# Layer 0's four product groups for the scans by quarters of the contraction beside the modulation, the gate product later, the modulation spread anew

## The chip, the core and the metric

The kernel runs on one core of a Trainium2 chip. The metric is the device time of one execution in microseconds (us), the median over a few executions. A difference of 0.3% (8.7 us) is about what a measurement of this kernel can tell from none.

## The reference, cut to what matters

Two layers run over two groups of 128 tokens each (context and latent) with shared weights; D_MODEL is 2048. The code is cut to the parts that the change touches.

```python
def _modulation(cond, ada_w, ada_b):
    m = jax.nn.silu(cond) @ ada_w + ada_b
    m = m.reshape(cond.shape[0], 1, N_MOD, D_MODEL)
    return [m[:, :, i] for i in range(N_MOD)]
...
def _mixer(h, p, ctx):
    u = h @ p['w_in']
    q, k, v, u_hy, u_rkv, w_dn, a_dn, g_dn = jnp.split(u, IN_SPLITS, axis=-1)
    ...
    hy = _hyena(u_hy, p)
    rw, S_fin = _rwkv(u_rkv, w_dn, a_dn, g_dn, p, S0)
    o = jnp.concatenate([att, hy, rw], axis=-1) @ p['w_out']
...
def _layer(x, cond, p, ctx):
    sh1, sc1, g1, sh2, sc2, g2 = _modulation(cond, p['ada_w'], p['ada_b'])
    nw = p['norm_w']
    h = _rmsnorm(x, nw[0]) * (1.0 + sc1) + sh1
    o, st = _mixer(h, p, ctx)
    x = x + g1 * _rmsnorm(o, nw[1])
    h = _rmsnorm(x, nw[2]) * (1.0 + sc2) + sh2
    f = jnp.square(jax.nn.relu(h @ p['mlp_w1'])) @ p['mlp_w2']
    x = x + g2 * _rmsnorm(f, nw[3])
```

The six modulation vectors of a layer (numbers 0 to 5: sh1, sc1, g1, sh2, sc2, g2) need one 2048 x 12288 weight matrix per layer, 16.8 MB a vector. The scans (`_rwkv`) need r, k, v and the two low-rank inputs of decay and rate (`w_dn`, `a_dn`); the gate input `g_dn` is used only at their end.

## The kernel before, in words

**Products.** A weight is loaded in float32 by SyncE's DMA queue, split by ScalarE (L244) and VectorE (L245) into two halves, and every product is three matmuls: high x high (seen as L165), high x low and low x high (L523 and L524 in `ws`, L542 and L543 in `as_`). `ws` holds the weight still and moves 256 tokens; `as_` holds the tokens still and moves up to 512 weight columns. One load covers two or four of the sixteen 128-row steps of the contraction. `self.run` drives such a group; each of its steps reports its columns, and 6144 columns are one **unit** (24 matmuls of 256 columns).

**Modulation.** `ada_vector` loads one vector as 32 tiles of 512 KB (L394) and multiplies each (L399). One tile with its matmuls is a **step**; a vector has 33 or 34. `ada_push` queues vectors, `run` issues so many steps per unit as `ada_mix` (in the mixer) or `ada_mlp` (in the MLP) says, `drain` issues one whenever the side work has to wait, `ada_until` issues what is left up to a vector, and `ada_step(fill)` issues `fill` more before the residual and norm that follow the mixer of each layer and the MLP of layer 0. Layer 0's vectors 1 and 0 are needed first. `ada_group` computes them in four column groups of 512, and `ada_boot` takes turns between two; the products of one vector's column group are eight tiles of 512 KB (L354, L360).

**Start.** In `build`, each column group of the two vectors releases a quarter of the norm (`norm`, one chunk of `act` per call) and, some steps later (`b1`, `b2`), four contraction steps of the two groups of `mixer_first`: "wa" (four blocks of 96 columns, the low-rank inputs) and "k" of the first half of the heads. These two groups hold the two PSUM buffers of the tag `mm` until the fourth quarter.

**Mixer.** `mixer` then runs, in this order: `rwkv_lora` and the short convolution of k (`conv`, L551 to L553), the gate group (C_G, 256 columns), r and v of the first half, then q, k, v of the attention, r, k, v of the second half, three Hyena groups and the output projection in three phases (attention with heads 0 and 1, Hyena, the rest). The scans are side work: `side.add(rwkv_batch ...)` stands after v; a batch of three pairs of heads goes through `rwkv_kk`, `rwkv_stage1`, `rwkv_invert` (a chain of VectorE steps with two round trips through DRAM), `rwkv_stage2` and `rwkv_out`, and the second batch follows the first. `Side.step` issues pieces of it as units go by. Before each phase of the output projection `drain` issues what the phase still needs. `Beside.queue` pins each side matmul behind the last product matmul issued, so that the planner cannot move it ahead; apart from that the planner orders each engine's queue by program order and by its own estimate of when operands are ready.

**Residual and norm.** After the output projection and after each MLP, `residual` (L1248, L478) and `norm` (L473, L487, L497 to L502) form a chain over VectorE, ScalarE and transposes (L179) before the next product can start.

**Buffers.** Raw weight tiles: four of the tag `wr` (products, and half of the first modulation tiles) and six of `wa` (modulation). Three high and three low halves. `sm` has three PSUM buffers, `mm` two.

Of the kernel before, what the change touches and what calls it, by code (L numbers as in the profile page):

```python
# [33 lines left out]
def _shape_constants():  # L34
# [56 lines left out]
    for k, v in c.items():  # L91
# [16 lines left out]
OPTS = dict(mm_bufs=2, sm_bufs=3, raw=4, araw=6, hi=3, lo=3, t0=16, t1=8, k1=25, k2=15, k4=18, ada_mix=1.0,  # L108
            ada_mlp=0.75, sr=3.5, sq=3, sh=4, so=7, ra=0.3, wa1=1.5, wa2=0.5, w0=1, w1=3, wi=0.5,
            ni=3, w2=0.5, w3=3, w4=2, w5=0.4, fill=8, b1=2, b2=5)  # L110
# [47 lines left out]
class Beside:  # L158


    def __init__(self, tc):
        self.tc, self.last = tc, None

    def main(self, *a, **k):
        i = self.tc.nc.tensor.matmul(*a, **k)  # L165
        self.last = i.ins.name
        return i

    def queue(self, i):
        if self.last is not None:  # L170
            self.tc.add_manual_dep(i.ins, self.last, mybir.DependencyInfo(mybir.DependencyClass.NoSync, mybir.DependencyReason.DATA),
                                   reason="beside")
        return i

    def matmul(self, *a, **k):
        return self.queue(self.tc.nc.tensor.matmul(*a, **k))  # L176

    def transpose(self, *a, **k):
        return self.queue(self.tc.nc.tensor.transpose(*a, **k))  # L179


class Kern:
    def __init__(self, tc, es, A, O, opts=None):
# [7 lines left out]
        self.te = Beside(tc)  # L191
# [8 lines left out]
    def late(self, ins, back=8):  # L200

        if len(self.anchors) > back:
            self.tc.add_manual_dep(ins.ins, self.anchors[-1 - back],
                                   mybir.DependencyInfo(mybir.DependencyClass.Sync, mybir.DependencyReason.DATA), reason="late")
        return ins

# [42 lines left out]
    def setup(self):  # L249
# [17 lines left out]
        self.te.transpose(ps[:, 0:32], th[:], self.ident[0:32, 0:32])  # L267
# [21 lines left out]
    def params(self, l):  # L289
# [34 lines left out]
        for i, gr in enumerate(groups):  # L324
# [3 lines left out]
            self.te.transpose(ps[:, 0:n], rows[:], self.ident[0:n, 0:n])  # L328
# [151 lines left out]
    def norm(self, P, parts, isc, ish, act):  # L480
# [3 lines left out]
        for c in range(4):  # L484
            for g in range(2):
# [4 lines left out]
                for j in range(4):  # L490
                    self.te.transpose(pv[:, j, :], xn[:, j * 128:(j + 1) * 128], self.ident)
# [14 lines left out]
    def ws(self, act, w, widths, ps):  # L506
# [4 lines left out]
        for kq in range(KT // nk):  # L511
            hi, lo = self.wload(w[kq * nk * 128:(kq + 1) * nk * 128, :], nk, ncol)
            for kk in range(nk):
                k = kq * nk + kk
                hh, hl = act[k // 4][0][:, k % 4, :], act[k // 4][1][:, k % 4, :]
                c0 = 0
                for b, wd in enumerate(widths):
                    o = ps[0:wd, b * 256:(b + 1) * 256]
                    h, lw = hi[:, kk, c0:c0 + wd], lo[:, kk, c0:c0 + wd]
                    m = self.te.main(o, lhsT=h, rhs=hh, start=(k == 0 and b % 2 == 0), stop=False, skip_group_check=True)  # L520
# [878 lines left out]
```

## Time and profile before

| | |
|---|---|
| median of three executions | 2912.18 us (2906.03 to 2915.72) |
| the profiled execution | 2905.54 us |
| its span, first to last instruction | 2903.8 us |
| TensorE (matmul) busy | 2798.7 us, 96% |
| VectorE, ScalarE busy | 57%, 42% |
| HBM read | 632.21 MB |

The profile is of one execution. In the view of windows a row gives the length of a stretch, then for each engine its busy time and instruction count, then TensorE's mean granted clock (1.00 is 2.4 GHz, 0.50 is 1.2 GHz), the mean busy share of the DMA engines and what they moved. In the timeline a row gives start, duration, engine, line, operation, output and inputs, shapes and count; the bracket is the time that the engine sat idle before it and what ended that. Each matmul of the modulation is float32 and shows as two instructions, so that one step shows as x4.

### The profile page before, as it was taken

How to read it: one execution, taken by the hardware profiler on the slowest of the kernel's cores; microseconds unless marked ns; L12 is line 12 of the kernel's file. 1: busy time of each engine (PE TensorE's matmuls, PEld its weight loads, DVE VectorE, ACT ScalarE, POOL GpSimd, SP SyncE). 2: the span in 40 equal slices, each digit the busy share in tenths (PEclk: the TensorE clock that was granted, in tenths of full speed). 3: DMA queues.
4: the chain of work that ended last, by engine and by line, in shares of the span. 5: the costliest groups of instructions: out<-in, count | busy, mean ns of one | idle time of the engine just before them, and what ended most of it. 6: DMA issues, size and time to landing. Idle time of an engine off the chain costs nothing. (4 is left out here: it accounts for less than half of the span.)

```text
span 2903.8 us, 47850 instructions
## 1 busy us (share of the span) xinstructions
PE 2798.7 (96%) x19163; PEld 2308.9 (80%) x19163; DVE 1646.6 (57%) x2627; ACT 1232.8 (42%) x1870; POOL 179.1 (6%) x368
## 2 busy tenths in 40 slices
PE   6899999999999999999999999999879999999998
PEld 3586888766897797897876979887669989899896
DVE  1356766776644344444445577677775545555555
ACT  2354445433533343333345454453354444444343
POOL 0011101201000000000000111021000000000000
PEclk8999999999999999999999999998989999999999
DMA  9985764578888888888898745433456666666674
GB/s 334 335 302 192 236 225 153 188 240 289 294 282 288 278 285 277 294 280 282 284 337 286 225 138 143 137 90 111 146 176 184 185 191 184 188 188 187 190 241 150
DMA packets 326057, 654.56 MB, mean 225 GB/s; under 512 B 48581, under 2 KB 86030, under 8 KB 325707
## 3 DMA queue, kind: packets, MB, share of 16 engines
q1 hardware_dynamic: 311328, 610.88, 65.0%
q0 software_dynamic: 12928, 36.98, 3.8%
q8 instruction: 150, 2.46, 0.3%
q10 hardware_dynamic: 1579, 3.64, 0.3%
q14 instruction: 72, 0.59, 0.1%
HBM read 632.21 MB, written 19.20 MB: 224 GB/s over the span
## 5 line engine op out<-in xcount | busy, mean ns | idle before, releaser
L245 DVE TENSOR_TENSOR wl<-wr,wh 128x1024 fp32r<-128x1024 f32 (+1 forms) x784 | 929.1, 1186 | 926.6 <-ACT wh L244 903.2
L244 ACT CAST wh<-wr 128x1024 fp32r<-128x1024 f32 (+1 forms) x784 | 798.6, 1019 | 1188.3 <-PE mm L523 532.9
L165 PE MATMUL mm<-acth,wh 128*128 128x256 f32 (+1 forms) x3200 | 922.0, 288 | 11.8 <-ACT acth L501 8.5
L523 PE MATMUL mm<-actl,wh 128*128 128x256 f32 (+1 forms) x3200 | 906.5, 283 | 0.0
L524 PE MATMUL mm<-acth,wl 128*128 128x256 f32 (+1 forms) x3200 | 904.5, 283 | 1.9 <-DVE wl L245 1.9
L165 PEld LDWEIGHTS mm<-acth,wh 128*128 128x128 f32 (+1 forms) x3200 | 603.6, 189 | 61.0 <-issue 25.2
L524 PEld LDWEIGHTS mm<-acth,wl 128*128 128x128 f32 (+1 forms) x3200 | 604.7, 189 | 7.2 <-DVE wl L245 3.5
L523 PEld LDWEIGHTS mm<-actl,wh 128*128 128x128 f32 (+1 forms) x3200 | 602.4, 188 | 4.1 <-issue 2.7
L165 PE MATMUL mm<-wh,fh 128*128 128x512 f32 x1024 | 405.8, 396 | 0.0
L542 PE MATMUL mm<-wl,fh 128*128 128x512 f32 x1024 | 403.0, 394 | 0.0
L543 PE MATMUL mm<-wh,fl 128*128 128x512 f32 x1024 | 401.6, 392 | 0.0
L165 PEld LDWEIGHTS mm<-wh,fh 128*128 128x128 f32 x1024 | 192.2, 188 | 63.0 <-ACT wh L244 9.2
L543 PEld LDWEIGHTS mm<-wh,fl 128*128 128x128 f32 x1024 | 192.0, 187 | 45.4
L542 PEld LDWEIGHTS mm<-wl,fh 128*128 128x128 f32 x1024 | 192.2, 188 | 42.5 <-DVE wl L245 0.4
L399 PE MATMUL ada<-wa,cs 128*32 128x512 f32 x1280 | 180.0, 607 | 6.7 <-DMA wa<-in_ada_w_dram 6.5
L165 PE MATMUL mm<-wh,osh 128*128 128x512 f32 x256 | 106.4, 416 | 4.9 <-ACT osh L1200 3.4
L542 PE MATMUL mm<-wl,osh 128*128 128x512 f32 x256 | 101.9, 398 | 0.3 <-DVE wl L245 0.3
L399 PEld LDWEIGHTS ada<-wa,cs 128*32 128x32 f32 x1280 | 35.5, 109 | 83.5 <-issue 55.4
L543 PE MATMUL mm<-wh,osl 128*128 128x512 f32 x256 | 101.3, 396 | 0.0
L176 PE MATMUL sm<-rZR,rKB 64*128 64x256 f32 x384 | 76.4, 419 | 1.4 <-DVE rLA L933 1.4
L165 PE MATMUL mm<-wh,acth 128*128 128x512 f32 (+1 forms) x192 | 74.4, 387 | 0.0
L542 PE MATMUL mm<-wl,acth 128*128 128x512 f32 (+1 forms) x192 | 68.8, 358 | 0.0
(319 smaller groups left out, 2566.5 us busy)
## 6 DMA issues: line engine op xcount, KB each, us to landing
wr<-in_mlp_w_dram SPq DMA_DIRECT2D x512, 512.0 KB
wa<-in_ada_w_dram SPq DMA_DIRECT2D x352, 512.0 KB
wr<-in_w_in_dram SPq DMA_DIRECT2D x96, 512.0 KB
wr<-in_w_in_dram SPq DMA_DIRECT2D x112, 384.0 KB
wr<-in_w_out_dram SPq DMA_DIRECT2D x64, 512.0 KB
wr<-in_ada_w_dram SPq DMA_DIRECT2D x32, 512.0 KB
gb<-gate POOLq DMA_DIRECT2D x16, 512.0 KB, 9.3
xd<-acc SPq DMA_DIRECT2D x24, 256.0 KB
```

The source lines that it names most:

```text
L165: i = self.tc.nc.tensor.matmul(*a, **k)
L176: return self.queue(self.tc.nc.tensor.matmul(*a, **k))
L244: nc.scalar.copy(hi, raw)
L245: nc.vector.tensor_sub(lo, raw, hi)
L399: nc.tensor.matmul(ps[32 * j:32 * j + 32, :], lhsT=self.cs[:, kk, :], rhs=w[2 * (kk - k + 1) + j // 2][:, 512 * (j % 2):512 * (j % 2) + 51 ...
L523: nc.tensor.matmul(o, lhsT=h, rhs=hl, start=False, stop=False, skip_group_check=True)
L524: nc.tensor.matmul(o, lhsT=lw, rhs=hh, start=False, stop=(k == KT - 1), skip_group_check=True)
L542: nc.tensor.matmul(o, lhsT=hh, rhs=lo[:, kk, :], start=False, stop=False)
L543: nc.tensor.matmul(o, lhsT=hl, rhs=hi[:, kk, :], start=False, stop=last)
```

## The change

`mixer_first` becomes one generator over four groups (wa, k, r, v of the first half). For each quarter c of the contraction each group runs four steps into a PSUM buffer, which is then copied (c = 0, ScalarE) or added (VectorE) into a float32 tile in SBUF, so the two `mm` buffers go round. In `build` the first three quarters are interleaved with the modulation's steps at `bo` = 1.2 of them to one product step; the last quarter runs in `mixer`. The convolutions of k, r and v and `rwkv_lora` read the SBUF tiles. In both layers the scans are added before the gate group instead of behind v, and the gate group comes after them. Layer 1's vectors 3 and 5 are queued in layer 1 instead of in layer 0's MLP; steps per unit become 1.0 and 0.35 in the mixers (1.0 in both before) and 0.6 and 0.1 in the MLPs (0.75 in both); `fill` becomes 16. The class `Beside` becomes two methods with the same dependency, which accounts for most of the diff's lines and is left out here.

```diff
-            ada_mlp=0.75, sr=3.5, sq=3, sh=4, so=7, ra=0.3, wa1=1.5, wa2=0.5, w0=1, w1=3, wi=0.5,
-            ni=3, w2=0.5, w3=3, w4=2, w5=0.4, fill=8, b1=2, b2=5)
+            ada_mlp=(0.6, 0.1), sr=3.5, sq=3, sh=4, so=7, ra=0.3, wa1=1.5, wa2=0.5, w0=1, w1=3, wi=0.5,
+            ni=3, w2=0.5, w3=3, w4=2, w5=0.4, fill=16, bo=1.2)
...
     def mixer_first(self, l, act):
...
         W = self.A["w_in"][l]
-        ps = self.mm(), self.mm()
-        return [(ps[0], self.ws(act, W[:, C_WA:C_WA + 384], [96] * 4, ps[0])),
-                (ps[1], self.ws(act, W[:, C_R + 768:C_R + 768 + 384], [128] * 3, ps[1]))]
+        F = self.F = {n: sb([128, 1024], F32, tag="f" + n) for n in ("wa", "k", "r", "v")}
+        cols = {"wa": (C_WA, [96] * 4), "k": (C_R + 768, [128] * 3), "r": (C_R, [128] * 3), "v": (C_R + 1536, [128] * 3)}
+        for c in range(4):
+            for n, (c0, widths) in cols.items():
+                ps = self.mm()
+                yield from self.ws(act, W[:, c0:c0 + sum(widths)], widths, ps, range(4 * c, 4 * c + 4))
+                dst, src = (x[0:widths[0], 0:256 * len(widths)] for x in (F[n], ps))
+                if c == 0:
+                    nc.scalar.copy(dst, src)
+                else:
+                    nc.vector.tensor_add(dst, dst, src)
+            yield None
...
-        self.run(first[0][1], 1, ada)
-        self.rwkv_lora(first[0][0], P)
-        self.run(first[1][1], 1, ada)
-        rkv_conv("k", 0, first[1][0])
+        if first is not None:
+
+            self.run(first, 1, ada)
+            self.rwkv_lora(self.F["wa"], P)
+            for nm in "krv":
+                rkv_conv(nm, 0, self.F[nm])
+        else:
+            ps = self.mm()
+            self.run(self.ws(act, W[:, C_WA:C_WA + 384], [96] * 4, ps), 1, ada)
+            self.rwkv_lora(ps, P)
+            rkv(0)
+        self.side.add(self.rwkv_batch(l, P, 0, u), self.rwkv_out(l, P, 0), self.rwkv_batch(l, P, 1, u), self.rwkv_out(l, P, 1))
         ps = self.mm()
         self.run(self.ws(act, W[:, C_G:C_G + 256], [128] * 2, ps), o["sh"], ada)
         self.rwkv_gate(ps, P)
-
-        rkv(0, "rv")
-        self.side.add(self.rwkv_batch(l, P, 0, u), self.rwkv_out(l, P, 0), self.rwkv_batch(l, P, 1, u), self.rwkv_out(l, P, 1))
...
-        while self.adaq or todo:
-            if self.adaq:
-                self.ada_boot()
+        n = 0
+        while len(self.adaq) > 6:
+            self.ada_boot()
             n += 1
...
+        for c in range(4):
+
+            next(norm)
+            if c < 3:
+                left, due = 2 * (2 - c), 0.0
+                for step in iter(lambda: next(first), None):
+                    due += self.o["bo"]
+                    while due >= 1 and len(self.adaq) > left:
+                        self.ada_boot()
+                        due -= 1
+                while len(self.adaq) > left:
+                    self.ada_boot()
...
-            if l > 0:
+            else:
+                self.ada_push(l, p, (3, 5))
...
-                self.ada_push(l + 1, P[l + 1], (1, 0, 2, 4, 3, 5))
+                self.ada_push(l + 1, P[l + 1], (1, 0, 2, 4))
```

## Rows read from the trace of the kernel before

**Rows 1.** The page: the span in 40 slices, TensorE, its clock, the DMA engines.

```profile
PE   6899999999999999999999999999879999999998
...
PEclk8999999999999999999999999998989999999999
DMA  9985764578888888888898745433456666666674
```

**Rows 2.** Windows: two rounds of the start, then what follows it.

```profile
49.90:78.80 28.90, 25.65 (x174) 16.82 (x174) 8.89 (x16) 8.00 (x14) 0.00 (x0) 0.94 0.99 346
78.80:108.00 29.20, 26.50 (x172) 15.90 (x172) 7.98 (x17) 7.34 (x13) 0.00 (x0) 0.94 0.93 338
...
134.20:148.70 14.50, 14.45 (x98) 14.04 (x98) 3.27 (x4) 6.56 (x9) 4.60 (x8) 0.80 1.02 332
148.70:208.00 59.30, 59.27 (x453) 49.25 (x453) 32.68 (x50) 27.57 (x38) 8.30 (x14) 1.00 0.87 284
```

**Rows 3.** The same windows, product matmuls alone.

```profile
78.80:108.00 29.20, 10.39 (x84) 0.94 0.93 338
...
134.20:148.70 14.50, 14.34 (x96) 0.80 1.02 332
148.70:208.00 59.30, 47.55 (x379) 1.00 0.87 284
```

**Rows 4.** DMA issues: form, count, KB each.

```profile
wa<-in_ada_w_dram SPq DMA_DIRECT2D x352, 512.0 KB
...
wr<-in_w_in_dram SPq DMA_DIRECT2D x112, 384.0 KB
```

**Rows 5.** Groups by line on VectorE: count, busy us, mean ns, idle before.

```profile
L1210 DVE TENSOR_TENSOR acc<-acc,mm 128x512 f32<-128x512 f32 x32 | 20.7, 682 | 9.4 <-PE mm L543 9.3
...
L552 DVE SCALAR_TENSOR_TENSOR ru_v<-mm,pv,ru_v 128x254 f32<-128x254 f32 x12 | 5.7, 479 | 5.6 <-ACT ru_v L551 5.5
```

**Rows 6.** Timeline: the last short convolution of v in layer 0's first half.

```profile
212.24 0.48 DVE L553 SCALAR_TENSOR_TENSOR ru_v<-mm,pv,ru_v 128x254 f32<-128x254 f32 x1
```

**Rows 7.** Timeline: TensorE's waits around the scans, layer 0, then layer 1.

```profile
682.33 3.67 PE L176 MATMUL sm<-rG,rLA 128*128 128x64 f32 x16 [4.37 <-ACT rsf L1057]
...
2066.90 0.50 PE L165 MATMUL mm<-wh,osh 128*128 128x512 f32 x1 [3.39 <-ACT osh L1200]
...
2074.34 0.81 PE L176 MATMUL sm<-rG,rXT 32*32 32x64 f32 x6 [6.94 <-DMA rXT<-rdout]
```

**Rows 8.** Windows of 10 us around those waits.

```profile
680.00:690.00 10.00, 7.67 (x48) 5.02 (x48) 4.27 (x12) 2.57 (x7) 4.34 (x8) 0.52 0.66 246
1980.00:1990.00 10.00, 8.21 (x46) 6.33 (x45) 9.19 (x20) 7.68 (x17) 0.00 (x0) 0.84 0.19 57
1990.00:2000.00 10.00, 10.00 (x33) 7.22 (x33) 3.27 (x10) 0.75 (x4) 0.00 (x0) 0.50 0.15 50
2070.00:2080.00 10.00, 5.66 (x59) 4.26 (x61) 1.24 (x3) 1.10 (x3) 0.00 (x0) 0.50 0.38 70
```

**Rows 9.** Timeline: modulation steps, and the norm's first transposes in layer 1.

```profile
715.09 1.92 PE L399 MATMUL ada<-wa,cs 128*32 128x512 f32 x16
...
722.88 1.05 PE L399 MATMUL ada<-wa,cs 128*32 128x512 f32 x4 [0.70 <-DMA wa<-in_ada_w_dram]
...
728.33 1.05 PE L399 MATMUL ada<-wa,cs 128*32 128x512 f32 x4 [0.84 <-DMA wa<-in_ada_w_dram]
...
1561.95 1.05 PE L399 MATMUL ada<-wa,cs 128*32 128x512 f32 x4 [2.40 <-DMA wa<-in_ada_w_dram]
...
2159.52 1.94 PE L179 MATMUL sm<-const,xn 128*128 128x128 f32 x8 [11.46 <-DVE rs L473]
```

**Rows 10.** Windows: layer 1's norm, the products behind it, the norm behind layer 0's MLP.

```profile
2148.10:2165.10 17.00, 3.06 (x12) 2.29 (x12) 13.68 (x31) 11.84 (x33) 0.00 (x0) 0.57 0.60 209
2165.10:2176.30 11.20, 11.19 (x71) 10.98 (x71) 8.53 (x18) 6.69 (x13) 0.00 (x0) 0.74 0.01 2
...
1556.80:1574.20 17.40, 11.72 (x57) 2.80 (x56) 13.66 (x31) 11.55 (x33) 3.43 (x7) 0.90 0.95 299
```

More of the change, by code (lines that the diff above doesn't have):

```diff
@@ L155, in step @@
         return any_
[L158 to L179, printed above, removed]
 class Kern:
@@ L190, in __init__ @@
         self.side = Side()
-        self.te = Beside(tc)
+        self.last = None
         self.adaq = deque()
@@ L205, in late, with product, beside @@
         return ins
+    def product(self, i):
+        self.last = i.ins.name
+        return i
+    def beside(self, i):
+        if self.last is not None:
+            self.tc.add_manual_dep(i.ins, self.last, mybir.DependencyInfo(mybir.DependencyClass.NoSync, mybir.DependencyReason.DATA),
+                                   reason="beside")
+        return i
     def wide(self, tag):
@@ L327, in params @@
             ps = self.sm()
-            self.te.transpose(ps[:, 0:n], rows[:], self.ident[0:n, 0:n])
+            self.beside(nc.tensor.transpose(ps[:, 0:n], rows[:], self.ident[0:n, 0:n]))
             pv = sb([128, n], F32, tag=f"pv{i}", bufs=2)
@@ L503, in norm, with ws @@
             yield
-    def ws(self, act, w, widths, ps):
+    def ws(self, act, w, widths, ps, ks=range(KT)):
         nc = self.nc
@@ L538, in as_ @@
                     o = ps[:, g * 512:g * 512 + ncol]
-                    m = self.te.main(o, lhsT=hh, rhs=hi[:, kk, :], start=first, stop=False)
+                    m = self.product(nc.tensor.matmul(o, lhsT=hh, rhs=hi[:, kk, :], start=first, stop=False))
                     if g == 0 and kk == 0:
@@ L595, in hyena_filter @@
         ps = self.sm()
-        self.te.matmul(ps[0:64, 0:128], lhsT=f2[:], rhs=h1[:], start=True, stop=True)
+        self.beside(nc.tensor.matmul(ps[0:64, 0:128], lhsT=f2[:], rhs=h1[:], start=True, stop=True))
         h2 = self.sin_(ps[0:64, 0:128], bb[:, 1:2], "hh2")
@@ L616, in hyena_filter @@
             ps = self.sm()
-            self.te.matmul(ps[:], lhsT=self.cst(m), rhs=src[:], start=True, stop=True)
+            self.beside(nc.tensor.matmul(ps[:], lhsT=self.cst(m), rhs=src[:], start=True, stop=True))
             H = sb([128, 512], F32, tag="hHs")
@@ L874, in rwkv_stage1 @@
         ps = self.sm()
-        self.te.matmul(ps[:, 0:256], lhsT=self.cst("bones"), rhs=rk[:], start=True, stop=True)
+        self.beside(nc.tensor.matmul(ps[:, 0:256], lhsT=self.cst("bones"), rhs=rk[:], start=True, stop=True))
         bv = sb([128, 256], F32, tag="rbv")
@@ L1119, in run @@
         for n in gen:
-            n /= 6144
+            n = (n or 0) / 6144
             self.side.now += n
@@ L1319, in build @@
         first = self.mixer_first(0, act)
-        n, cg, todo = 0, 0, deque()
-        def products():
-            for _, g in first:
-                for _ in range(4):
-                    next(g)
-        while self.adaq or todo:
-            if self.adaq:
-                self.ada_boot()
+        n = 0
+        while len(self.adaq) > 6:
+            self.ada_boot()
             n += 1
@@ L1336, in build @@
                 norm = self.norm(P[0], next(rest), 1, 0, act)
-            if cg < 4 and len(self.adaq) < 2 * (4 - cg) - 1:
-                todo.append((n + self.o["b1"], lambda: next(norm)))
-                todo.append((n + self.o["b2"], products))
-                cg += 1
-            while todo and (todo[0][0] <= n or not self.adaq):
-                todo.popleft()[1]()
+        for c in range(4):
[9 more added lines that the diff above has]
+                    self.ada_boot()
         for l in range(DEPTH):
@@ L1351, in build @@
                     pass
-                first = self.mixer_first(l, act)
-            acc, ss = self.mixer(l, p, act, first)
+            acc, ss = self.mixer(l, p, act, first if l == 0 else None)
             self.ada_until(l, 3)
```

87 lines of the change are left out of this document (44 added, 43 removed).

## Prediction

> **What bounds the kernel now.** I began with the slices of the page [rows 1]: TensorE is at nine tenths or more in all but the first and two others, so the kernel is bound by the work on TensorE, none of which this change takes away. What can be won is only where TensorE stands still or runs at its low clock. The slices show where: the first two (the start, DMA engines at nine tenths), the one near 710 us, and the ones near 2060 and 2150 us, where the clock digit falls to 8 and 9 too. So I read three places: the start by windows, the waits around the scans by the timeline, and the norms between mixer and MLP by both.
>
> At the start a round of 28.9 us (one column group of vectors 1 and 0 with a quarter of wa and k) has the DMA engines at 0.99 and TensorE busy for 25.65 [rows 2]. Its loads are 16 tiles of 512 KB and four of 384 KB [rows 4], 9.96 MB, and 346 GB/s times 28.9 us is 10.0 MB: the round is as long as its loads take. Behind the start, from 148.7 us on, TensorE has no gap and the DMA engines are at 0.87.
>
> Around the scans TensorE waits 4.37 us in layer 0, and 3.39 and 6.94 us in layer 1 [rows 7]. The last is for `rXT`, the second round trip of the second batch's inversion: the scans are late there. Stretches at the low clock go with such waits: 0.52, 0.50 and 0.50 [rows 8]. In layer 1's norm TensorE stands for 11.46 us [rows 9] and has 3.06 us of work in 17.0 [rows 10].
>
> The sum is made against the profiled execution, 2905.54 us, whose span is 2903.8. It lies 6.6 us below the median of 2912.18; I take the difference off the median.
>
> **Part 1, the start.** Each of three rounds gets a quarter of r and v more: four loads of 384 KB, 1.57 MB, to 11.53 MB. At 342 GB/s (the mean of the two rounds) that is 4.6 us a round, 13.8 us for three, and the last quarter starts at 148.0 instead of 134.2. TensorE gets 72 matmuls more a round (156 instead of 84), at 0.124 us each [rows 3] 8.9 us. Added to its 26.50 busy that would be 35.4, 6.2 more than the round of 29.2 and 18.6 for three; this is the upper end, since its busy time holds modulation steps that are stretched by waiting for tiles. The lower end is 8: 338 GB/s at a DMA share of 0.93 would be 363 at a full one, 31.7 us a round. I take 13.8, as the first round stands at 0.99.
>
> Against that, 216 matmuls (three quarters of r and v) are no longer done behind the start. There 379 take 47.55 us and 84 take 10.39, about 0.12 each, so 25.9 us go. The start gives 25.9 - 13.8 = **12.1 us**, between 7 and 18. The steps of layer 0's modulation that rode on those nine units are done later at the same cost. The low clock of the last quarter (0.80, 14.34 us for 96 matmuls) stays: the chain from the last modulation tile over the norm to `act` is the same.
>
> The four evacuations of a round are priced by the add of 128x512, 0.68 us [rows 5]: 1.0 for each group of 768 columns, 1.4 for wa, 4.4 us on a VectorE that is busy for 8 to 9 of 29 us. They cost nothing as long as the other `mm` buffer keeps TensorE fed. Behind the last group stand an add and three convolutions of v, on VectorE 1.0 + 6 x 0.48 = 3.9 us, with the copies on ScalarE between them some 5; the gate's 96 matmuls, 11.5 us, lie beside. If the halves of the gate's weights queue behind them, TensorE waits up to those 5 us. SyncE's queue carries the same loads in another order.
>
> **Part 2, the scans.** In layer 0 the last convolution of v ends at 212.7 [rows 6]. Now: 148.0 + 156 x 0.12 + 3 for the low clock + 5 = 175, so the first batch starts 38 us earlier, by the order of the products one gate group earlier. What this can win there is the wait of 4.37 and what 7.67 us at 0.52 lost [rows 8], 3.7 (busy time times what is missing to 1.00). The wait followed loads that were late, so I take **3 us**, between 0 and 8. In layer 1 the scans start one gate group, 11.5 us, earlier, and the products between them and the wait (78 units: attention, second half, Hyena, first phase) get 0.35 x 78 = 27 modulation steps of 0.48 us (1.92 for four [rows 9]), 13 us, beside which the chain goes on. That is more than the 6.94. At stake are 10.3 of waits, 2.8 lost in 2070 to 2080 and 1.3 + 5.0 in 1980 to 2000, 19.4 in all. I take **12 us**, the two waits and part of the clock, between 0 and 19. Late next would be `rwkv_out` and the norm.
>
> **Part 3, the norms.** The modulation's work is the same; what counts is how much of it falls where TensorE stands. (a) Behind layer 0's MLP 0.6 x 256 = 154 steps are issued, and only some 145 are queued (135 for vectors 1, 0, 2 and 4, and the rest of layer 0's), so nothing is left to fill with. There are now 11.72 us of work in 17.4 [rows 10], eleven steps among them: 5.3 us move to where TensorE is busy. I take **5 us lost**, between 0 and 6. (b) Layer 1's norm gets up to 16 steps. Tiles come at 1.8 us each (722.88 to 728.33, three steps [rows 9]), six lie ready, so some twelve fit beside the chain: 5.8 us. The clock there is 0.57, and 0.74 behind it, which costs 11.19 x 0.26 = 2.9 us; behind layer 0's MLP, with such steps, it is 0.90. I take **7 us** for both, between a loss of 7 and a gain of 9. The Trainium skill, "TensorE: Matmul & The Clock Gate", in its section on oscillation, says that short bursts of matmuls between waits for DMA let the clock fall again each time. By that rule the gain here would be 6 instead of 7; the trace speaks against it with 0.90 where steps come one by one. (c) Layer 0's norm gets 16 instead of 8. Eight more are 3.8 us gained if they fit, 14.5 lost if the transposes queue behind them. I take 0.
>
> **Sum.** -12.1 - 3 - 12 + 5 - 7 = -29.1: 2876 for the profiled execution, **2883 us** as a median. With all ends together -58 to about +19, 2854 to 2931.
>
> **The rivals.** *A, slower: the modulation holds what it should cover.* TensorE takes its queue in order, as its waits show [rows 7], where it stands 6.94 us for a tile of the scans with products behind it, so a step whose tile has not landed holds the transposes or the scans behind it. Place: the norms and layer 1's drains. For it: waits of 0.70 and 2.40 us for tiles [rows 9]. Against it: the first of those rows has four steps without any wait. Price: layer 0's norm 14.5; layer 1's norm 10 steps x 1.8 = 18 instead of 11.5, 6.5; a drain of 20 steps, of which 14 come at 1.8, 25 instead of the 10.3 of waits, 15. With -12.1 - 3 + 5 that gives +26, 2938. It decides from about 15 steps that wait: (10 + 8.7) divided by 1.8 - 0.48.
>
> *B, the start gives nothing.* If loads and TensorE hold each other up through the four `wr` tiles, which products and half of the modulation share, a round becomes 8.6 longer and all 25.9 are used up: -17, 2895. For it: 35.4 us of TensorE in a round of 33.7. Against it: TensorE's busy time there is stretched.
>
> *C, no change.* The pieces of the scans are released as units go by, so an earlier start need not make them end earlier; the wait stays, the start gives 7, the norms lose 5: -2, 2910. For it: the second batch cannot start before the second half's products. Against it: layer 0, which has modulation steps beside its scans, shows no wait for `rXT`. That r and v only push modulation aside, so that the change does not do what it says, ends here too.
>
> **How the numbers follow.** Forecast 0.55, B 0.17, C 0.14, A 0.14. Below 2903 (0.3%, 8.7 us, what a measurement can tell) lie the forecast and B but for their slow ends: faster 0.70; C and those ends: same 0.16; slower 0.14. The range leaves out A and the last of the fast tail: 2854 (all gains at their ends) to 2912 (takes in C).
>
> **What would show it.** Right: the last quarter starts near 148 and the gate ends near 195 instead of 207; DMA at 0.95 or more in the rounds; no wait for `rXT` in layer 1; steps of L399 in layer 1's norm and a clock above 0.57 there; none behind layer 0's MLP. Wrong: the last quarter past 160; VectorE ahead of a long wait for `wl` at the gate; waits for `wa` tiles just before transposes of the norm, or in layer 1 between phases.

## The result, and the profile after

The changed kernel takes 2939.44 us in the median of 12 executions (2921.63 to 2950.67), the kernel before 2916.62 beside it (12 executions, 2902.12 to 2927.85): ratio 1.008, 95% interval 1.0056 to 1.0104, so 16 to 30 us slower. The profiled execution took 2935.49 us, its span is 2933.7; the one of before 2903.8.

The page's slices of the changed kernel, TensorE, its clock and the DMA engines:

```profile
PE   6889999999999999999998999999989999999998
...
PEclk8999999899999999999999999999999999999999
DMA  8884775377888878787897646634686666666674
```

Beside [rows 1] TensorE's two weak slices near 2060 and 2150 us rose from 8 and 7 to 9 and 8. But the third slice fell from 9 to 8 (and one near 1580 us, the norm behind layer 0's MLP), and the DMA digits of the start fell from 9985 to 8884. So the start comes first. The windows of its three rounds, then of what follows, up to where ScalarE has read the gate group (columns as in [rows 2]):

```profile
48.60:93.30 44.70, 40.39 (x248) 26.58 (x248) 11.65 (x19) 13.84 (x22) 0.00 (x0) 0.92 0.82 282
93.30:136.30 43.00, 37.97 (x244) 24.62 (x244) 16.04 (x24) 11.09 (x17) 0.00 (x0) 0.96 0.81 274
136.30:176.90 40.60, 35.91 (x238) 23.91 (x238) 16.56 (x25) 11.00 (x18) 4.59 (x8) 1.00 0.91 311
176.90:206.60 29.70, 27.81 (x196) 22.38 (x196) 19.16 (x38) 18.89 (x29) 2.51 (x4) 0.94 0.74 248
206.60:236.90 30.30, 27.30 (x151) 19.84 (x152) 16.49 (x24) 14.39 (x25) 7.10 (x12) 0.94 0.80 272
```

A round lasts 42.8 us in the mean, where it lasted 28.1 ([rows 2], and a third of 26.2). The DMA engines' share is 0.81 to 0.91 instead of 0.93 to 0.99, and TensorE's busy time isn't the round either. The last quarter starts at 177.0 instead of 134.2. The products alone in the same rounds, against 10.39 for 84 [rows 3]:

```profile
48.70:93.35 44.65, 24.37 (x156) 21.62 (x157) 0.00 (x0) 3.40 (x4) 0.92 0.82 282
93.35:136.40 43.05, 22.09 (x157) 19.66 (x157) 4.08 (x4) 0.00 (x0) 0.96 0.81 274
136.40:177.00 40.60, 21.25 (x157) 19.00 (x157) 4.07 (x4) 0.00 (x0) 1.00 0.91 312
```

Who waits is seen in the view of waits (engine, line, released by: us in all, times, longest). In the rounds of the changed kernel the split on ScalarE waits for product weights, and SyncE's queue stands at loads (L342 is a modulation tile, L231 a product weight) whose buffer is still in use:

```profile
ACT wh L232 <- DMA wr<-in_w_in_dram: 60.2, 15, 9.4
```

```profile
SPq L342 <- PE sm L348: 24.9, 6, 5.2
SPq L342 <- DVE wl L233: 21.7, 8, 4.4
SPq L342 <- DMA wr<-in_w_in_dram: 13.5, 8, 2.4
SPq L231 <- DVE wl L233: 12.7, 8, 3.6
```

In the rounds of the kernel before the first of these was

```profile
ACT wh L244 <- DMA wr<-in_w_in_dram: 2.2, 3, 1.3
```

So the product weights come late now. That SyncE's queue stands is not new, though: in the rounds of the kernel before it stood at loads without a buffer for 59.4 of 84.3 us (L354 is the modulation tile there, L243 a product weight), in the changed one for 85.0 of 128.3.

```profile
SPq L243 <- PE sm L360: 20.7, 11, 4.8
SPq L354 <- DVE wl L245: 15.1, 12, 3.8
```

The last product of the set "wa, k, r, v, gate", in the kernel before (v's) and in the changed one (the gate's):

```profile
204.25 0.28 PE L524 MATMUL mm<-acth,wl 128*128 128x256 f32 x1
```

```profile
231.67 0.28 PE L512 MATMUL mm<-acth,wl 128*128 128x256 f32 x1
```

It starts 27.4 us later, of the 29.9 by which the span grew (the medians lie 22.8 apart). Some 3.3 us of that are pieces of the scans, done earlier than before. What follows takes 2933.7 - 231.7 = 2702.0 us, where it took 2903.8 - 204.3 = 2699.5. The loss is the start; the rest gained nothing.

### The profile page after: what moved, and what is told of

It reads as the page before. It is cut to its first block, busy times and chain, and to the rows that moved or that the text cites. A ratio compares the mean times of both kernels' runs of the same rounds, so it can differ in the third digit from the quotient of the medians.

```text
span 2933.7 us, 47858 instructions
## 1 busy us (share of the span) xinstructions
PE 2832.3 (97%) x19163; PEld 2307.9 (79%) x19163; DVE 1659.0 (57%) x2639; ACT 1234.2 (42%) x1874; POOL 179.0 (6%) x368
## 5 line engine op out<-in xcount | busy, mean ns | idle before, releaser
L508 PE MATMUL mm<-acth,wh 128*128 128x256 f32 (+1 forms) x3200 | 923.7, 289 | 12.9 <-ACT acth L489 8.7
L387 PE MATMUL ada<-wa,cs 128*32 128x512 f32 x1280 | 197.4, 625 | 21.9 <-DMA wa<-in_ada_w_dram 21.1
L917 PE MATMUL sm<-rZR,rKB 64*128 64x256 f32 x384 | 87.6, 438 | 1.2 <-DVE rLA L921 0.9
```

The costliest lines, as they stand in the source:

```text
L387: nc.tensor.matmul(ps[32 * j:32 * j + 32, :], lhsT=self.cs[:, kk, :], rhs=w[2 * (kk - k + 1) + j // 2][:, 512 * (j % 2):512 * (j % 2) + 51 ...
L508: m = self.product(nc.tensor.matmul(o, lhsT=h, rhs=hh, start=(k == ks[0] and b % 2 == 0), stop=False, skip_group_check=True))
L917: self.beside(nc.tensor.matmul(ps[h][:, i * 256:(i + 1) * 256], lhsT=KB[hs, d, g, i, :], rhs=ZR[hs, d, g, :, :].rearrange("p i t -> p (i t ...
```

## The experiments

Times are medians with their ratio to the kernel before on the same chip; rounds, waits and clocks are those of the one profiled execution of each run.

**Where the loss is.** `e3_oldstart` has the start and layer 0's order of before; the rest is as changed.

```diff
+        if self.o["old"]:
+            ps = self.mm(), self.mm()
+            return [(ps[0], self.ws(act, W[:, C_WA:C_WA + 384], [96] * 4, ps[0])),
+                    (ps[1], self.ws(act, W[:, C_R + 768:C_R + 768 + 384], [128] * 3, ps[1]))]
...
```

> The changed kernel with the start and layer 0's order of the kernel before (wa and k by quarters, then gate, r, v, then the scans); layer 1's order and the new spread of the modulation stay. If the start is what costs (28 us by the landmark of gate, r and v done: 236.9 instead of 208), this is 25 to 30 us faster than the changed kernel and within 0.3% of the kernel before (ratio 0.997 to 1.003), since behind the start the two traces take 2683 and 2682 us. If the spread and the order of the scans cost as well, it stays 0.4% or more above the kernel before; if they gain, as was predicted, it is at 0.994 or below.

Measured: 2916.28, ratio 0.9992 (0.9974 to 1.001). All of the loss that can be measured is in the start and layer 0's order; layer 1's order and the new spread together are worth nothing that can be measured. `e8_order` also takes back the spread:

```diff
-ada_mix=(1.0, 0.35), ada_mlp=(0.6, 0.1) ... fill=16
+ada_mix=(1.0, 1.0), ada_mlp=(0.75, 0.75) ... fill=8
...
-                self.ada_push(l, p, (3, 5))
...
-                self.ada_push(l + 1, P[l + 1], (1, 0, 2, 4))
+                self.ada_push(l + 1, P[l + 1], (1, 0, 2, 4, 3, 5))
```

> e3_oldstart with the spread of the modulation of before as well, so that against the kernel before only layer 1's order of scans (gate product behind r and v) is left of the change. If that order is worth what the prediction gave it (12 us) and the new spread costs it back: 2902 to 2908. If neither is worth anything: 2914 to 2919. If the order costs and the spread pays: 2920 to 2928.

Measured: 2920.03, ratio 1.0011 (0.9992 to 1.0029): neither is worth anything that can be measured. Here the same 4154 matmul instructions of layer 1's mixer stand in both traces, first to last product; before, then `e8_order`:

```profile
1574.20:2148.10 573.90, 553.82 (x4154) 468.03 (x4154) 410.92 (x832) 273.14 (x505) 70.91 (x147) 0.97 0.50 152
```

```profile
1580.70:2159.00 578.30, 562.68 (x4154) 471.56 (x4154) 412.52 (x832) 272.20 (x505) 70.67 (x147) 0.97 0.49 151
```

The waits of 3.39 and 6.94 us [rows 7] are gone in `e8_order`, and TensorE's waits in all fell from 21.9 to 16.9 us; yet the stretch is 4.4 us longer. The time that matmuls hold the queue (from the start of one to the start of the next, less the waits shown) went from 168.5 to 177.0 us for the scans and the other small matmuls, and from 379.2 to 380.1 for the products. The scans' last matmuls do come sooner, 542.4 us into the stretch instead of 553.4 (before, then `e8_order`):

```profile
2127.59 1.03 PE L176 MATMUL sm<-rsg,rgu 128*128 128x256 f32 x4
```

```profile
2123.09 1.13 PE L1081 MATMUL sm<-rsg,rgu 128*128 128x256 f32 x4
```

So the scans were earlier and waited less, and no time was won. I read the 8.5 us as TensorE's standing, spread over their small matmuls; no run shows that.

**Small pieces?** In the rounds of the changed kernel some 64 modulation instructions take 12.9 to 14.3 us, in about ten pieces; before, 64 took 10.3 and 12.5 in four. `e1_pairs` begins each pair of tiles with the newer one, so that a piece has one wait:

```diff
-                for j in range(4):
+                for j in (2, 3, 0, 1):
```

> The changed kernel, but the four matmuls of a pair of the first modulation tiles are issued with those of the later tile first, so that all four become ready together and stand next to each other in TensorE's queue. Theory S (split: matmuls of the modulation on different column groups overlap only when they are next to each other; the interleaving cut them into pieces of two and four instructions, each about 1 us, 14 us a round for 64): a round falls from 42.8 us by 3 to 5, the last quarter starts at 162 to 168 instead of 177, and the kernel gains about 10 us on the changed one (ratio to before near 1.004). Theory L (loads: products and half of these tiles share the four wr buffers in one load queue, and the DMA engines stand still for them at a share of 0.81): rounds stay within 1.5 us of 42.8.

Measured: 2934.5, ratio 1.0071 (1.0048 to 1.0094). The modulation's time in a round fell to 10.7 to 12.8 us, but the waits rose from 3.8 to 5.5 us a round to 7.0 to 9.4, and the rounds are 44.9, 44.4 and 46.6 (in the slowest of its six executions, 2947.64). `e2_burst` gives the modulation no place between the products (`bo=0.0`), so that it comes in one block:

> The changed kernel with no modulation step between the products of a quarter: all sixteen product steps of the four groups in one burst, the round's modulation behind them. Theory S: pieces of the modulation are long again as in the kernel before, a round is that of before (28.9) plus 72 matmuls (8.9), about 38, last quarter at about 163. Theory L: while the burst of 19 us runs, eight product loads go through four buffers and modulation fills only the rest, so the DMA share stays at or below 0.85 and a round at 40 or more.

Measured: 2922.73, ratio 1.0011 (0.9992 to 1.003); rounds of 42.0, 43.9 and 42.4. It is 17 us faster than the changed kernel with rounds no shorter: what it gained came behind them (from the last quarter to the last product of the set 49 us instead of 55, the rest 2696 instead of 2702), and why isn't settled. The pieces alone are not what makes a round long. The same order in the later modulation, in the kernel before (`e6_before_whole`) and in `e3_oldstart` (`e7_oldstart_whole`):

```diff
-                    for kk in (k - 1, k):
-                        for j in range(4):
+                    for kk in (k, k - 1):
+                        for j in (2, 3, 0, 1):
...
```

> The kernel before, with the later modulation's matmuls of a pair of tiles in another order: the newest tile first and its columns before the other's, so that the pair's sixteen instructions stand behind one wait instead of two. Theory P (a modulation instruction in the mixers and norms costs .17 us rather than .123 because it is put down in pieces that each wait for a split): the modulation's time behind the start falls from 164 us by 5 to 15 us, time 2902 to 2911. Theory N (the pieces wait for loads or for the clock, and the order does not matter): 2914 to 2919.

> The kernel with the start and layer 0's order of before, and the changed kernel's order in layer 1 and its spread (e3_oldstart: 2916, ratio .9992), with the same newest-first order of the modulation's pairs. Here 168 modulation instructions stand in layer 1's mixer at .17 us each and 64 in its norm. Theory P: they come down to .12 to .13 us, 8 to 15 us in all, time 2901 to 2908, faster than the kernel before and than e6. Theory N: 2914 to 2919.

Measured: 2920.72, ratio 1.0007 (0.9993 to 1.002), and 2918.58, ratio 1.0004 (0.9986 to 1.0021). In layer 0's mixer and norm the modulation's time did fall, from 63.8 to 57.3 us in the first and from 71.7 to 61.6 in the second, and TensorE's waits rose there from 18.7 to 24.5 and from 13.3 to 27.2. Theory N holds: the wait for a tile was there anyway, and stands now ahead of the piece instead of within it.

**Buffers.** `e4_more` gives the low half of the first modulation's tiles buffers of their own instead of `wr`:

```diff
-            t = sb([128, 2, 512], F32, tag=tag, bufs=self.o[{"wr": "raw", "wa": "araw"}[tag]])
+            if tag == "wr":
+                t = sb([128, 2, 512], F32, tag="boot")
+            else:
+                t = sb([128, 2, 512], F32, tag=tag, bufs=self.o["araw"])
```

> The changed kernel, but the first modulation's tiles no longer use the wr buffers: those that did take free buffers of another class (two and more at that time), so products have wr for themselves and more loads can be under way. Theory L: DMA share of the rounds rises from 0.81 to 0.95 or more, a round falls to 34 to 36, last quarter at about 155. Theory S: rounds stay within 1.5 us of 42.8, as the pieces are cut by the order of the queue and not by late tiles.

Measured: 2926.22, ratio 1.0044 (1.0024 to 1.0065); rounds of 41.1, 41.5 and 38.2, 2.5 us shorter in the mean. Shared tiles are a part of it, a small one: no split in these rounds waits for product weights any more, where such waits added up to 60.2 us in the changed kernel, and yet the rounds are hardly shorter. ScalarE now stands 31.8 us at the copy of the modulation's row (arow) instead. `e5_pool` issues these loads from GpSimd's queue as well:

```diff
-            nc.sync.dma_start(t[:], A["ada_w"][l, kq * 256:(kq + 1) * 256, c0:c0 + 512] ...
+            nc.gpsimd.dma_start(t[:], A["ada_w"][l, kq * 256:(kq + 1) * 256, c0:c0 + 512] ...
```

> The run with the first modulation's low halves in buffers of their own (e4_more: 2926, last quarter from 172.9 us, rounds 41 us, DMA share .80), with the first modulation's ada_w loads issued from GpSimd's queue, so that one of them that waits for a buffer no longer holds the product loads behind it on SyncE's. Theory Q (one queue for both kinds of loads is what keeps the transfers at .8): DMA share of the rounds .9 or more, rounds of 36 us or less, last quarter from 160 us or earlier, time 2912 to 2916. Theory L (a round is a loop run one after the other: last modulation tile, row, norm, ScalarE's copy, products; the queue only follows it): rounds stay at 40 to 42 us, share about .8, last quarter at 170 to 174, time 2923 to 2929. If GpSimd's own work (it makes halves of the split and the norm) holds the loads back instead: rounds over 43 us, time over 2930.

Measured: 2922.58, ratio 1.0017 (0.9994 to 1.0041); rounds of 40.6, 37.8 and 42.0 at shares of 0.83 to 0.85. Theory Q fell, and theory L's figures nearly came: the last quarter starts at 174.7. As in `e4_more` no split waits for weights; the mean round is 40.1 us against 40.3. This profile is of the slowest of ten executions (2939.56). By the ratios, 1.0044 and 1.0017, the second queue gives some 8 us in all, but their intervals overlap. Its second round, and what the two queues wait for in the rounds (a split to free a product buffer, TensorE to free a modulation tile):

```profile
94.89:132.73 37.84, 35.53 (x244) 25.46 (x244) 15.34 (x24) 10.91 (x16) 10.19 (x15) 0.86 0.85 309
```

```profile
SPq L231 <- DVE wl L233: 77.1, 18, 11.7
```

```profile
POOL wa L345 <- PE sm L351: 55.7, 7, 17.2
```

**How much is moved.** `e9_none` keeps the new way of working but computes r and v whole behind the last quarter (84 products a round, as before); `e10_half` so computes only v (120).

```diff
+                if n in ("v",) and c < 3:
+                    continue
                 ps = self.mm()
-                yield from self.ws(..., ps, range(4 * c, 4 * c + 4))
+                yield from self.ws(..., ps, range(0 if n in ("v",) else 4 * c, 4 * c + 4))
...
```

> The changed kernel with its start's way of working (quarters into PSUM, copied or added into SBUF, modulation between the product steps), but with r and v computed whole behind the last quarter, so that a round has the 84 products of before instead of 156 (modulation steps per product step 2.4, so that the same number lies between; half as many later modulation steps beside the last quarter). Theory M (a round gets longer by what is added to TensorE): rounds of 29 to 31 us, last quarter at 136 to 143, time 2914 to 2921. Theory I (the interleaving itself costs: modulation in small pieces, evacuations, tiles shared): rounds of 34 us or more, last quarter past 152, time 2925 or more.

> As the run before, but only v is computed behind the last quarter: 120 products a round, half of what the change adds (1.6 modulation steps per product step). Theory M: rounds half way between those of e9_none and of the changed kernel (42.8), about 36, and the time half way too, 2926 to 2930: every product moved costs as much there as it saves behind, or more. Theory S (TensorE has slack of some 3 us a round, used up first): rounds of 31 to 33, time 2908 to 2914.

Measured: 2926.58, ratio 1.0036 (1.0014 to 1.0058), rounds of 33.2, 32.6 and 33.4; and 2943.22, ratio 1.0077 (1.0052 to 1.0103), rounds of 44.0, 40.7 and 40.4. The new way costs 4.9 us a round by itself, without one product moved. Half of the products then cost as much as all of them: this is no sum of work, and `e10_half` is no faster than the changed kernel because it saves half as much behind. `e11_half_more` adds the buffers of `e4_more`:

> As e10_half, with the low halves of the first modulation in buffers of their own (e4_more, which gave 13 us with all of the products moved). If buffers are what half of the products lacks: rounds 31 to 33, time 2908 to 2914, the only start that could beat the old one. By theory M: rounds 34 to 36, time 2917 to 2923.

Measured: 2943.6, ratio 1.0088 (1.0057 to 1.0119); rounds of 43.5, 42.6 and 43.0. Buffers alone change nothing here. Its second round, and its queue:

```profile
93.89:136.46 42.57, 37.61 (x208) 23.35 (x209) 12.59 (x21) 8.71 (x15) 0.00 (x0) 0.88 0.60 210
```

```profile
SPq L345 <- PE sm L351: 59.2, 9, 16.8
SPq L231 <- DVE wl L233: 28.7, 8, 9.2
```

The DMA engines are at 0.60 while SyncE stands 59 us in all at modulation tiles (L345) that have no buffer, with product weights queued behind them. But the splits hardly wait for those weights (1.6 us here, 36.6 in `e10_half`); ScalarE stands at the row copy instead:

```profile
ACT arow L356 <- PE sm L351: 43.0, 6, 14.7
ACT wh L232 <- DMA wr<-in_w_in_dram: 1.6, 1, 1.6
```

**What each side takes alone.** `e12_noload` loads 2 of the first modulation's 64 tiles; `e14_noprodload` loads all 64 and lets the products of the four groups read one tile.

```diff
-            t = sb([128, 2, 512], F32, ...)
-            nc.sync.dma_start(t[:], A["ada_w"] ...)
+            if kq % 2 not in self.bw:
+                self.bw[kq % 2] = sb([128, 2, 512], F32, tag="boot")
+                nc.sync.dma_start(self.bw[kq % 2][:], A["ada_w"] ...)
+            t = self.bw[kq % 2]
```

> e4_more with 2 instead of 64 tiles of ada_w loaded for the first modulation (every product of it reads one of these two, so its values are not those of the reference); products, norm and evacuations are the same. Rounds there: 41.2, 41.5, 38.3. Theory Loads (the loads set the pace, by bandwidth or by buffers): rounds of 35 us or less. Theory T (TensorE's own row of work, with the low clock behind each norm, is the round): 37 to 40 us with the transfers nearly idle, DMA share below .5, and TensorE busy for over .93 of them.

> The counterpart of e12_noload: the changed kernel in which the products of the four groups all read one tile that is loaded once (so their values are not those of the reference), while all 64 modulation tiles are loaded as in the changed kernel, alone on the queue and in ten buffers; the splits, products, norm and evacuations stay. By the transfers a round is 8.39 MB, 24 us at 345 GB/s; by TensorE's row of e12_noload it is 33. Theory Q (the two kinds of loads hold each other up): 33 to 35 us. Theory B (ten buffers for the modulation's tiles, each freed only when TensorE gets to it between products, are too few): 38 us or more.

Measured: rounds of 32.7, 33.5 and 33.6, one execution 2877.21; and 34.1, 33.7 and 33.7, one execution 2909.31. Windows of the rounds, `e12_noload`, then `e14_noprodload`, and the latter's queue (L350 is the modulation tile there):

```profile
49.70:82.40 32.70, 32.70 (x261) 23.41 (x260) 11.63 (x20) 13.68 (x20) 0.00 (x0) 1.00 0.58 180
82.40:115.90 33.50, 33.50 (x268) 23.60 (x267) 15.44 (x23) 10.91 (x16) 0.00 (x0) 1.00 0.53 168
```

```profile
49.23:83.35 34.12, 32.92 (x254) 23.41 (x254) 14.22 (x22) 15.12 (x22) 0.00 (x0) 1.00 0.75 268
83.35:117.09 33.74, 32.23 (x246) 23.41 (x245) 15.43 (x24) 10.91 (x16) 0.00 (x0) 0.95 0.80 281
```

```profile
SPq L350 <- PE sm L356: 51.3, 15, 9.7
```

TensorE with all 156 products, the modulation and the norm needs 33.3 us and stands still in neither of the two rounds shown. With the modulation's loads in ten buffers it needs 33.9: the queue stands 51 us at tiles without a buffer, and that costs 0.6 us a round at most, with no product weights queued behind them. Theory T fell (its 37 to 40 held the waits), and so did theory B. With both kinds of loads a round takes 42.8 us in one queue, and 40.1 in two (`e5_pool`). So it takes both kinds to make a round long, but these two runs don't say by what: each takes away bytes and claims on buffers along with a share of the queue, and the planner put TensorE's work in another order. Behind the last transposes of a norm, where TensorE waits for the next quarter, `e12_noload` has 26 modulation matmuls ready and `e5_pool` four:

```profile
112.34 3.62 PE L351 MATMUL sm<-boot,cs 128*32 128x512 f32 x26
```

```profile
130.01 1.92 PE L351 MATMUL sm<-boot,cs 128*32 128x512 f32 x4
```

**Two queues at half of the products.** `e13_half_pool` is `e11_half_more` with the edit of `e5_pool`; `e15_pool_pairs` and `e16_half_pool_pairs` are `e5_pool` and `e13_half_pool` with the order of `e1_pairs`.

> e11_half_more with the first modulation's loads on GpSimd's queue (as e5_pool, with v behind the last quarter). Rounds of e11: 43.5, 42.6, 43.0, with SyncE's queue held for 59 us by modulation tiles without a buffer. Theory Q (a load that waits for a buffer holds the product loads behind it in the one queue, which is why half of the products cost as much as all): rounds of 31 to 35 us, time 2910 to 2920. Theory B (the buffers of the modulation tiles set the pace, on whichever queue): rounds stay over 38, time over 2928.

> e5_pool (rounds 40.6, 37.8, 42.0; TensorE busy for .93 of the first two at a clock of .88 and .86) with the matmuls of a pair of tiles in the order that begins with the newer tile, as in e1_pairs, where the modulation's time fell by 3 us a round and the waits rose by as much. If TensorE's row is what is left of e5_pool's round: 35 to 37 us, time 2913 to 2919. If its loop with the loads is: rounds within 1 us of e5_pool's, time 2920 to 2926.

> e13_half_pool with the order of e15_pool_pairs: the best start that the runs so far allow. Theory Q: rounds of 30 to 33 us, time 2905 to 2914, so equal to the kernel before or faster. Theory B: rounds over 37, time over 2926.

Measured: `e13_half_pool` 2927.56, ratio 1.0051 (1.0033 to 1.0069), rounds of 36.0, 34.9 and 33.0:

```profile
52.98:88.94 35.96, 33.78 (x208) 21.21 (x209) 9.91 (x19) 11.31 (x17) 12.78 (x18) 0.88 0.93 341
88.94:123.81 34.87, 31.16 (x208) 21.05 (x208) 12.66 (x21) 9.14 (x14) 11.45 (x16) 0.92 0.81 305
123.81:156.82 33.01, 30.86 (x224) 20.50 (x224) 13.58 (x21) 9.14 (x14) 6.04 (x10) 0.95 0.82 292
```

```profile
POOL wa L345 <- PE sm L351: 51.7, 9, 16.1
```

The same tiles wait for buffers nearly as long as in `e11_half_more`, on another queue, and a round falls from 43.0 to 34.6. That is theory Q's range, but not shown to be by its reason, as the splits of `e11_half_more` waited only 1.6 us for weights. The edit also let the planner order the engines' work anew: in the second round TensorE has the modulation in 9 pieces instead of 13, and ScalarE has one of the six splits behind the two row copies instead of three. So ScalarE's waits in the rounds are others:

```profile
ACT wh L232 <- PE mm L514: 56.2, 17, 5.8
ACT arow L356 <- PE sm L351: 7.8, 6, 2.5
```

Fewer pieces changed little by themselves (`e2_burst`, and `e16_half_pool_pairs` below); no run holds ScalarE's order fixed. And the 8.4 us a round are of one execution each, that of `e13_half_pool` the fastest of twelve (2920.65): the medians lie 16.0 us apart, where three times 8.4 would be 25. The time of `e13_half_pool` missed (2910 to 2920 expected), as I left out that its rounds are 6.5 longer than before's, 19.5 in three, against 13 saved behind, and that its first round starts 3 us later. `e15_pool_pairs`: 2920.46, ratio 1.0016 (1.0 to 1.0033), rounds of 39.6, 37.1 and 38.5, nearer its second theory than its first. `e16_half_pool_pairs`: 2928.02, ratio 1.0046 (1.0027 to 1.0065), rounds of 37.9, 33.6 and 33.5; the order gives nothing, and the best start so far missed its 2905 to 2914. With all of the products two queues don't bring the round to 34. Against `e12_noload` a round of `e5_pool` has 3.0 us more for the same products (at clocks of 0.86 to 0.91 instead of 1.00), 2.3 more of waits and 1.5 more for the rest; one of `e15_pool_pairs` 2.6, 3.3 and 0.7 less. What makes these is open: buffers, the order of the queues behind the norm, or DMA engines at 0.85. No run that does the same work beats the kernel before.

| kernel | products a round | mean round, us | last product of the set at, us |
|---|---|---|---|
| before | 84 | 28.1 | 204.3 |
| changed | 156 | 42.8 | 231.7 |
| `e4_more` | 156 | 40.3 | 228.1 |
| `e5_pool`, `e15_pool_pairs` (two queues) | 156 | 40.1, 38.4 | 229.3, 224.0 |
| `e9_none` | 84 | 33.0 | 222.7 |
| `e10_half`, `e11_half_more` | 120 | 41.7, 43.0 | 230.4, 237.2 |
| `e13_half_pool` (two queues) | 120 | 34.6 | 215.6 |
| `e12_noload`, `e14_noprodload` | 156 | 33.3, 33.9 | 198.6, 205.5 |

## Why the prediction was wrong

**Part 1, the step that failed: "the round is as long as its loads take".** I put 33.7 us for the loads beside 35.4 for TensorE and let the loads set the round, as two things that run beside each other. Measured are 42.8. TensorE's figure was about right by itself: 33.3 us without the modulation's loads (`e12_noload`), and 33.9 with them and without the products' (`e14_noprodload`). The 33.7 for both kinds of loads no run has alone. So neither side by itself makes the round, and together they hold each other up. Against `e12_noload` a round of the changed kernel has 4.1 us more of waits, 3.2 more for the modulation and small matmuls, and 2.2 more for the products (21.7 instead of 19.4, at clocks of 0.92 to 1.00 instead of 1.00).

By what they hold each other up is shown in part only. The two kinds of loads share one queue, which stops at a load without a buffer. A modulation tile's buffer comes free when TensorE has gone through its place in the order, now set between product steps; behind it in the queue stand the weights of those product steps, and in the changed kernel the splits waited 60.2 us for weights. But tiles with buffers of their own ended that wait and gave 2.5 us a round (`e4_more`). A second queue gave 8.4 more at half of the products (`e11_half_more` against `e13_half_pool`, in their profiles), and 0.2 at all of them (`e4_more` against `e5_pool`; 1.9 with the order of `e15_pool_pairs`). What makes the larger part of the 9.5 us between the changed kernel and `e12_noload` stays open. The rival that no run rules out is the order of work in TensorE's and ScalarE's own queues, which the planner changed with each of these edits.

The Trainium skill, "DMA: Bandwidth & Descriptors", section "Issuing engines are not separate DMA queues", says that issuing from several engines saves only the time a sequencer takes to initiate a transfer. With all of the products the measurement nearly agrees (40.3 and 40.1 us a round); with half of them it is 8.4 us a round away from it, and the measurement decides, though by which path these were saved isn't shown.

The second term, 25.9 us no longer done behind the start, netted only 15.4: from the last quarter to the last product of the set it took 70.1 us and now 54.7. 216 fewer products show, for 24.4 us, close to what I gave; but 4.8 us of waits, 3.3 of scan pieces and 1.0 of modulation came in, which my sum had at nothing. So without any trouble in the rounds the start would have given next to nothing: `e14_noprodload` has the last quarter at 150.8, close to my 148.0, and its last product of the set at 205.5, where before had it at 204.3. For -12.1 stands +27.4, or +24.1 without the scan pieces; `e3_oldstart` against the changed kernel says 23.2.

The ends that I gave for what the three rounds gain in length, 8 and 18.6 us (measured: 44), both came from rounds in which the DMA engines hardly stood still (0.93 and 0.99), and neither had a price for the other order of the loads. I wrote that SyncE's queue carries the same loads in another order and left it at that, at nothing.

**Part 2, the scans.** Forecast -15; of this the -12 of layer 1 measured nothing (`e8_order`: -2.3 to +8.5 us), and layer 0's -3 was not measured by itself. The waits went, as forecast; what was wrong is that a wait that goes is time won. The 21.9 us of waits in layer 1's mixer fell by 5.0, and the scans' matmuls took 8.5 more. This is rival C's result without its reason, that the pieces need not end earlier: they ended 11 us earlier. In layer 0 the last convolution of v ends at 209.0 instead of 212.7, so the scans could start 4 us earlier and not 38, as the last quarter came so late.

**Part 3, the norms.** Windows of the changed kernel: layer 0's norm, the one behind layer 0's MLP, layer 1's, and the products behind that:

```profile
753.60:771.10 17.50, 13.94 (x69) 3.30 (x68) 13.93 (x31) 11.90 (x33) 0.00 (x0) 0.80 0.98 370
1577.50:1595.60 18.10, 9.80 (x49) 3.44 (x48) 14.71 (x34) 12.00 (x33) 2.82 (x5) 0.79 0.93 320
2171.30:2191.90 20.60, 12.04 (x57) 2.96 (x56) 16.28 (x33) 13.87 (x38) 0.00 (x0) 0.83 0.94 308
2191.90:2203.00 11.10, 11.02 (x79) 10.85 (x80) 9.11 (x19) 7.62 (x16) 0.00 (x0) 0.85 0.76 292
```

Layer 0's norm in the kernel before:

```profile
719.90:736.40 16.50, 9.40 (x49) 2.51 (x48) 13.95 (x31) 11.72 (x33) 3.94 (x8) 0.93 0.97 351
```

(a) Steps were not used up behind layer 0's MLP: some are still there, and the norm is 18.1 instead of 17.4 [rows 10] with two steps (1.0) fewer, so 1.7 lost instead of 5. (b) Layer 1's norm has its steps, and the clock rose from 0.57 to 0.83 and behind it from 0.74 to 0.85, as forecast in kind. But its tiles came late and the transposes stood behind them:

```profile
2180.37 6.63 PE L387 MATMUL ada<-wa,cs 128*32 128x512 f32 x18 [6.29 <-DMA wa<-in_ada_w_dram]
2186.93 0.66 PE L479 MATMUL sm<-const,xn 128*128 128x128 f32 x4
```

From last to first product there are 20.6 us instead of 17.0. Eleven steps of 0.48 moved in (5.3) and 11.1 us at 0.11 more of the clock (1.2), less 3.5, make a gain of 3 instead of 7. Rival A's mechanism is at work in this one place, at about half the price that I gave it there (3.5 us longer, not 6.5). By the rule of the Trainium skill, "TensorE: Matmul & The Clock Gate", section on oscillation, the clock falls again between short bursts; the trace agrees in part, with 0.79 to 0.83 in the three norms, under the 0.90 that I set against it and the 0.93 of layer 0's norm before. (c) Layer 0's norm went from 16.5 to 17.5 us with 20 instructions more, five steps or 2.4 us of work: 1.4 us gained, 0 forecast. These three rest on one execution each, and `e3_oldstart`, which has layer 0's order of before, bounds layer 1's scans and the norms together by -7.6 to +2.9 us against my -14.

**The rivals.** The time of A, 2938, came out nearly to the microsecond, and that is chance: its place was the norms and layer 1's drains. The place was B's, "loads and TensorE hold each other up": I let it use up what was saved and no more, 8.6 us a round, where it took 14.7. Nothing bounded it at that; with B priced from below only, no slower case was left at the start. Of the four shared `wr` tiles that I named for it, `e4_more` shows 2.5 us a round; what the rest is, no run shows. Of the signs for right, the wait for `rXT` that went and the steps and the clock in layer 1's norm held; of those for wrong, the last quarter past 160 and the wait for a `wa` tile just before the norm's transposes came, while VectorE's waits behind the last quarter stayed at 6.0 us at the longest. Two readings of mine were off without bearing on this: five slices of the page stand under nine tenths, not three, and the one near 710 us isn't among them [rows 1]; and the slow ends of the sum add up to +20.5, not +19.

## What to carry to other kernels

Before work is moved beside other work, look at the queue through which both get their data: if it is in order and either kind of load can stand waiting for a buffer, don't take the longer of the two times, however well each fits alone. Follow one load that waits and list what is queued behind it, and then look whether the engines really wait for that: here a 60 us wait vanished and the round fell by 2.5. Giving the two kinds separate queues is a cheap test, but where a planner orders the engines' work, compare that order before and after each edit, or the test changes two things. A wait that vanishes from a chain's view is won time only if the whole stretch, with the same count of instructions, gets shorter.

## What the runs showed of the hardware that I had not expected

Half of the moved products made a round as long as all of them (41.7 and 42.8 us), and none of them still 33.0 against 28.1: the length was no sum of the work. Putting the same modulation matmuls into larger pieces shortened their own time by up to 10 us and lengthened TensorE's waits by about as much (`e6_before_whole`, `e7_oldstart_whole`), so I read the duration that a matmul shows here as holding a part of the wait for its operands, and a mean per instruction (0.12 us in the first row of [rows 9], 0.21 in the changed kernel's rounds) is not its cost.
